# A decoder block on one core: where the rotation tables are worked out and which queues move the gate rows

## The chip, the cores and the metric

One core of a Trainium2 chip (trn2) runs the whole program. The metric is device time in microseconds (us), as the median of three runs of the kernel. Engines are named as in the profile: PE (TensorE, matrix products), DVE (VectorE), ACT (ScalarE), POOL (GpSimd) and SP (SyncE, which here only issues DMAs). Each engine works through its own queue of instructions in order and waits there for what an instruction needs; DMAs are issued from the queues of SP, ACT and POOL.

## The reference

One layer of a decoder, for 512 tokens of width 1024. The parts that matter here:

```
mod = silu(c) @ w_ada + b_ada            # six rows of 1024: shift, scale, gate, twice
h = rms_norm(x, norm1_g) * (1.0 + scale1) + shift1
z = h @ w_in                             # u, v, q, k, v, indexer q, k, weights, two gates
...
def partial_rope(x, pos, rot_dim):
    inv_freq = ROPE_THETA ** (-arange(0, rot_dim, 2) / rot_dim)
    ang = pos[..., None] * inv_freq
    cos, sin = jnp.cos(ang), jnp.sin(ang)
    ...                                  # rotate the first rot_dim columns of each head
...
x = x + gate1 * (merged @ w_out)
h2 = rms_norm(x, norm2_g) * (1.0 + scale2) + shift2
f_g, f_u = jnp.split(h2 @ w_ffn_in, 2, axis=-1)
x = x + gate2 * ((jax.nn.silu(f_g) * f_u) @ w_ffn_out)
return rms_norm(x, final_norm_g)
```

The rotation is applied to q, k and to the queries and keys of the indexer, which come out of the first products. The angles are positions times frequencies, brought into the range of the sine by taking off multiples of two pi. The gates are rows of 1024 numbers; each is used by all tokens.

## The kernel before, in words

Every product is computed with the operands split into a high and a low half (`hi`, `lo`), as three matmuls: high by high, high by low, low by high. ACT makes the high half by a copy, VectorE or POOL the low half by a subtraction.

**Order of the work.** The program is written out by hand in the order in which each engine shall take its instructions; nothing reorders them. `stream` is a list of weight chunks (`add_w`) and of rows of `w_ada` (`add_m`), in the order in which they are used. `ensure(n)` issues the loads of entries as far as their buffers allow (three raw chunks ahead, eight rows of `w_ada` ahead) and prepares entries up to n: for a weight chunk the high half (line 125) and the low half (129, or later through `do`, line 127), for a row of `w_ada` a dot product with silu(c) on VectorE (line 196), whose sum lands in a column of shifts, scales or gates.

**Prologue (lines 453 to 494).** ACT takes silu of `c`; PE spreads it over all partitions into two PSUM banks (`pc`); VectorE copies them to `scb` in SBUF (line 480). For each of the four token tiles ACT sums the squares of x (471), POOL makes the reciprocal root (356, 357), the first 256 columns are scaled (477 on VectorE, 475 on ACT for the last tile) and transposed by PE. The row factors are also spread over a bank, which ACT copies to `rbs` (490).

**First loop (lines 498 to 532).** It runs over the eight 128-row pieces kt of the transposed, modulated input, and accumulates k and six tiles of q in the eight PSUM banks. For piece kt PE does 8 matmuls high by high (512), 8 low by high (514) and 8 with the low half of the input (516), which VectorE makes at line 499. Beside them the next piece is prepared: VectorE scales it with `rbs` (504) and takes its two dot products (196); ACT multiplies the scale by the norm's gain (446, `stage_G`) and forms the high half and the full piece (450, 451, `stage_E`); VectorE then takes the low half of the weights (127). `load_xk` brings in the pieces themselves, four ahead.

**Rotation angles.** `chain` (lines 366 to 381) is a list of 26 operations on a tile of 128 by 128 (`ropes`), all on POOL, issued in one go ahead of the loop (`run_chain`, line 486). `sines()` (388), called at the end of kt = 1, makes two more operations on VectorE (389, 390) and three sines on ACT (391 to 393). Behind it POOL issues the 26 DMAs that spread the sines over the tables `tab_i` and `tab_q` (399, 402, 532).

**Middle part.** The remaining input products, the indexer's scores and the choice of keys, the two mixers and their projections; `w_ada`'s further rows are taken along between weight chunks.

**Gate rows.** When the eight dot products of a gate section (2 or 5) are done, `sec_tasks` (419 to 433) transposes the column of sums on PE, copies it on ACT (430), writes it to DRAM (`gdr`, 431) and reads it back as a row for all partitions (`gate`, 433); both DMAs are on POOL's queue. For section 2 this falls into the gate projections, at about 262 us, for section 5 into step 10 of the FFN loop.

**Later parts.** After attention, `opt_b` with `W_PB` and, woven into it, the preparation of the output product (`o_issue`, `o_step`); the output product with the first gated residual; the FFN's input products in 18 steps (lines 1603 to 1679), each with loads issued two steps ahead by SP (`s_issue`); and the last product (`zprod`), whose weights are sums of blocks that POOL's queue builds in DRAM during the FFN loop by accumulating DMAs (`wstep`, 298 and 300).

## Time and profile before

| | |
|---|---|
| median of 3 runs | 802.95 us (802.52 to 804.84) |
| profiled execution | 804.23 us |
| its span on the core | 802.5 us |
| PE busy | 783.7 us (98%) |
| DVE busy | 647.2 us (81%) |
| ACT busy | 424.0 us (53%) |
| POOL busy | 194.4 us (24%) |
| mean granted clock of TensorE | 0.989 |
| moved by DMA | 144.60 MB, mean 180 GB/s |

The span runs from the first instruction to the last on the core; the device time of the same execution is a little longer. A busy share is a mean over stages with different limits, and PE's matmuls are pipelined with modelled ends, so 98% does not say that PE works at its peak. In a row of the timeline stand the start and the length in us, the engine, the line of the kernel, the operation, what it writes and reads, and, where the engine stood idle before it, for how long and whose end released it. A row of the waits gives the waiting instruction, the one that it waited for, the total in us, the number of waits and the longest. A row of the stretches gives busy time and number of instructions of each engine, the granted clock, the mean share of the DMA engines and what they moved.

### The profile page before, as it was taken

How to read it: one execution, taken by the hardware profiler on the slowest of the kernel's cores; microseconds unless marked ns; L12 is line 12 of the kernel's file. 1: busy time of each engine (PE TensorE's matmuls, PEld its weight loads, DVE VectorE, ACT ScalarE, POOL GpSimd, SP SyncE). 2: the span in 40 equal slices, each digit the busy share in tenths (PEclk: the TensorE clock that was granted, in tenths of full speed). 3: DMA queues.
4: the chain of work that ended last, by engine and by line, in shares of the span. 5: the costliest groups of instructions: out<-in, count | busy, mean ns of one | idle time of the engine just before them, and what ended most of it. 6: DMA issues, size and time to landing. Idle time of an engine off the chain costs nothing.

```text
span 802.5 us, 12218 instructions
## 1 busy us (share of the span) xinstructions
PE 783.7 (98%) x4599; PEld 692.2 (86%) x4599; DVE 647.2 (81%) x1074; ACT 424.0 (53%) x755; POOL 194.4 (24%) x236
## 2 busy tenths in 40 slices
PE   8799999999999999999999999999999999999996
PEld 6579988888888888988888889999999999878885
DVE  5585967698888848887697778989999888798886
ACT  5446545332232327665636477555566566566653
POOL 6851043463344421000010000312221223100001
PEclk8899999999999999999999999999999999999998
DMA  9865454332346571138692603888989887656753
GB/s 362 346 201 146 112 174 123 106 94 90 105 158 208 189 232 53 53 108 264 207 246 42 209 1 105 231 238 267 269 250 244 217 219 208 185 189 201 231 181 142
DMA packets 87181, 144.60 MB, mean 180 GB/s; under 512 B 6737, under 2 KB 54625, under 8 KB 86930
## 3 DMA queue, kind: packets, MB, share of 16 engines
q1 hardware_dynamic: 75040, 111.92, 42.5%
q0 software_dynamic: 11216, 30.88, 16.4%
q10 hardware_dynamic: 866, 1.02, 0.4%
q8 instruction: 36, 0.59, 0.3%
q14 instruction: 23, 0.19, 0.1%
HBM read 139.73 MB, written 25.17 MB: 205 GB/s over the span
## 4 chain that ended last, share of the span: by engine, by line
PE 77%; DVE 8%; ACT 5%; DMA 4%; POOL 3%; issue 2%; SPq 0%; POOLq 0%; DVEq 0%; ACTq 0%
PE pb L67 8%; PE pb L66 8%; PE pb L68 8%; PE R L66 6%; PE R L68 6%; PE R L67 6%; PE pfo L67 3%; PE pfo L66 3%; PE pfo L68 3%; PE pgb L66 2%; PE pgb L67 2%; PE pgb L68 2%; PE pav L66 2%; PE pav L67 2%; PE pav L68 2%
## 5 line engine op out<-in xcount | busy, mean ns | idle before, releaser
L125 ACT ACTIVATE hi<-raw 128x1024 fp32r<-128x1024 f32 (+1 forms) x105 | 107.8, 1029 | 91.3 <-PE pb L67 20.9
L129 DVE TENSOR_TENSOR lo<-raw,hi 128x1024 fp32r<-128x1024 f32 (+2 forms) x69 | 80.5, 1168 | 28.7 <-ACT hi L125 28.6
L129 POOL TENSOR_TENSOR lo<-raw,hi 128x1024 fp32r<-128x1024 f32 x29 | 73.3, 2529 | 91.0 <-ACT hi L125 60.2
L66 PE MATMUL pb<-h,hi 128*128 128x512 f32 (+1 forms) x176 | 67.4, 383 | 0.0
L68 PE MATMUL pb<-h,lo 128*128 128x512 f32 (+1 forms) x176 | 66.8, 379 | 0.0
L67 PE MATMUL pb<-h,hi 128*128 128x512 f32 (+1 forms) x176 | 66.8, 379 | 0.0
L67 PE MATMUL pfo<-lo,za 128*128 128x512 f32 (+1 forms) x144 | 55.8, 388 | 1.4 <-DVE lo L129 1.4
L66 PE MATMUL pfo<-hi,za 128*128 128x512 f32 (+1 forms) x144 | 55.4, 384 | 0.0
L68 PE MATMUL pfo<-hi,za 128*128 128x512 f32 (+1 forms) x144 | 55.3, 384 | 0.0
L196 DVE CUSTOM_DVE_ANT_0 mraw<-mraw,scb,cols 128x1024 f32<-128x1024 f32 x27 | 39.3, 1457 | 15.0 <-DMA mraw<-in_w_ada_t_dram 15.0
L66 PE MATMUL R<-tb,sx 128*128 128x256 f32 x160 | 45.0, 281 | 0.6 <-ACT R L1637 0.3
L67 PE MATMUL R<-tb,sx 128*128 128x256 f32 x160 | 44.3, 277 | 0.0
L68 PE MATMUL R<-tb,sx 128*128 128x256 f32 x160 | 44.2, 276 | 0.0
L68 PE MATMUL R<-tb,lo 128*128 128x256 f32 x160 | 44.2, 276 | 0.0
L66 PE MATMUL R<-tb,hi 128*128 128x256 f32 x160 | 44.2, 276 | 0.0
L67 PE MATMUL R<-tb,hi 128*128 128x256 f32 x160 | 44.2, 276 | 0.0
L318 POOL COPY sm<-sm 128x1 f32<-128x1 f32 x36 | 23.7, 659 | 78.6 <-ACT sm L317 78.6
L298 POOL DMA_DIRECT2D wsum<-in_w_ffn_out_dram x24 | 21.2, 884 | 82.4 <-DMA wsum<-wsum 46.7
L68 PEld LDWEIGHTS pb<-h,lo 128*128 128x128 f32 x176 | 33.0, 188 | 5.7
L66 PEld LDWEIGHTS pb<-h,hi 128*128 128x128 f32 x176 | 33.1, 188 | 5.5
L67 PEld LDWEIGHTS pb<-h,hi 128*128 128x128 f32 x176 | 33.1, 188 | 5.3
L67 PEld LDWEIGHTS pfo<-lo,za 128*128 128x128 f32 x144 | 27.1, 188 | 8.3 <-DVE lo L129 3.2
(375 smaller groups left out, 2571.7 us busy)
## 6 DMA issues: line engine op xcount, KB each, us to landing
raw<-in_w_ffn_in_dram SPq DMA_DIRECT2D x44, 512.0 KB, 6.0
raw<-in_w_in_dram SPq DMA_DIRECT2D x38, 512.0 KB, 3.7
wsum<-in_w_ffn_out_dram POOLq DMA_DIRECT2D x30, 512.0 KB, 7.6
mraw<-in_w_ada_t_dram SPq DMA_DIRECT2D x27, 512.0 KB, 3.6
raw<-wsum SPq DMA_DIRECT2D x20, 512.0 KB, 4.0
s<-in_w_ada_t_dram SPq DMA_DIRECT2D x16, 512.0 KB, 8.8
raw<-in_w_ffn_out_dram SPq DMA_DIRECT2D x16, 512.0 KB, 4.4
wsum<-wsum POOLq DMA_DIRECT2D x10, 512.0 KB, 6.0
```

Source lines behind the costliest of these rows:

```text
L66: T.matmul(o, wh, rh, start=start, stop=False, **kw)
L67: T.matmul(o, wh, rlo, start=False, stop=False, **kw)
L68: T.matmul(o, wlo, rh, start=False, stop=stop, **kw)
L125: A.activation(hi[:, :m], e["raw"][:, :m], AF.Copy)
L129: e["lo"].tensor_sub(lo[:, :m], e["raw"][:, :m], f(hi[:, :m]))
L196: V.tensor_tensor_reduce(out=raw, in0=raw, in1=scb, scale=1.0, scalar=bias, op0=OP.mult, op1=OP.add, accum_out=col)
L298: P.dma_start(wsum[n][o], src, accum_op=OP.add)
L318: P.tensor_copy(t, t)
```

## The change

- The chain of rotation angles runs on VectorE, not POOL. The seven pairs of multiply and add become one fused operation each, and the two operations of `sines()` join the chain, which so has 21 entries. It is no longer issued in one go: four entries ahead of the first tile's scaling, four and three behind the first and second tile's, then 4, 4 and up to 8 at the ends of kt = 0, 1 and 2.
- `sines()` and the table DMAs come at the end of kt = 3, not 1.
- The first dot product reads silu(c) from the two PSUM banks, as two halves; the second half takes the first one's sum as its start. `scb` is copied by ACT, in the turn of the fourth tile, and no longer by VectorE. The first dot product is issued in the turn of the third tile.
- The copy to `rbs` stands between the two operations of `stage_E(0)`, no longer ahead of `stage_G(0)`.
- A gate row is written to DRAM from ACT's queue, in `sec_tasks`. It is read back from SP's queue by a function of its own, `gate_fetch`: for section 2 after attention, ahead of `o_issue`, for section 5 at the end of step 12 of the FFN loop.

```diff
@@ -187,14 +187,17 @@
     Gc = tiny.tile([128, 2, 16], F32, name="Gc")
     GG = {2: tiny.tile([128, 8], F32, name="GG2"), 5: tiny.tile([128, 8], F32, name="GG5")}
 
+    pc = []
+
     def dot(sec, kt, col, bias, after=lambda: None):
 
         def dma(raw):
             SY.dma_start(raw, w_ada_t[sec * D + kt * 128:sec * D + (kt + 1) * 128, :])
 
         def fn(raw):
-            V.tensor_tensor_reduce(out=raw, in0=raw, in1=scb, scale=1.0, scalar=bias, op0=OP.mult, op1=OP.add,
-                                   accum_out=col)
+            for o, c in ((slice(0, 512), pc[0]), (slice(512, D), pc[1])) if (sec, kt) == (0, 0) else ((slice(0, D), scb),):
+                V.tensor_tensor_reduce(out=raw[:, o], in0=raw[:, o], in1=c, scale=1.0,
+                                       scalar=col if o.start else bias, op0=OP.mult, op1=OP.add, accum_out=col)
             after()
         return dma, fn
 
@@ -365,20 +368,21 @@
     posf, ang, nh, nl, t0 = R[:, 0], R[:, 1], R[:, 2], R[:, 3], R[:, 4]
     chain = []
     ch = chain.append
-    ch(lambda: P.tensor_copy(posf, posi))
-    ch(lambda: P.tensor_scalar(ang, posf, freq, None, op0=OP.mult))
-    ch(lambda: P.tensor_scalar(nl, ang, float(1.0 / (2 * math.pi)), MAGIC, op0=OP.mult, op1=OP.add))
-    ch(lambda: P.tensor_scalar(nl, nl, -MAGIC, None, op0=OP.add))
-    ch(lambda: P.tensor_scalar(nh, nl, MAGIC * 2048.0, None, op0=OP.add))
-    ch(lambda: P.tensor_scalar(nh, nh, -MAGIC * 2048.0, None, op0=OP.add))
-    ch(lambda: P.tensor_sub(nl, nl, nh))
+    ch(lambda: V.tensor_copy(posf, posi))
+    ch(lambda: V.tensor_scalar(ang, posf, freq, None, op0=OP.mult))
+    ch(lambda: V.tensor_scalar(nl, ang, float(1.0 / (2 * math.pi)), MAGIC, op0=OP.mult, op1=OP.add))
+    ch(lambda: V.tensor_scalar(nl, nl, -MAGIC, None, op0=OP.add))
+    ch(lambda: V.tensor_scalar(nh, nl, MAGIC * 2048.0, None, op0=OP.add))
+    ch(lambda: V.tensor_scalar(nh, nh, -MAGIC * 2048.0, None, op0=OP.add))
+    ch(lambda: V.tensor_sub(nl, nl, nh))
     for pi, which in ((0, nh), (0, nl), (1, nh), (1, nl), (2, nh), (2, nl), (3, nh)):
-        ch(lambda pi=pi, which=which: P.tensor_scalar(t0, which, -TWO_PI[pi], None, op0=OP.mult))
-        ch(lambda: P.tensor_add(ang, ang, t0))
+        ch(lambda pi=pi, which=which: V.scalar_tensor_tensor(ang, which, -TWO_PI[pi], ang, op0=OP.mult, op1=OP.add))
     for cmp, sgn in ((OP.is_gt, -1.0), (OP.is_lt, 1.0)):
-        ch(lambda cmp=cmp, sgn=sgn: P.tensor_scalar(t0, ang, -sgn * math.pi, sgn * 2 * math.pi, op0=cmp, op1=OP.mult))
-        ch(lambda: P.tensor_add(ang, ang, t0))
-    ch(lambda: P.tensor_scalar(ang, ang, 3.1415925, -3.1415925, op0=OP.min, op1=OP.max))
+        ch(lambda cmp=cmp, sgn=sgn: V.tensor_scalar(t0, ang, -sgn * math.pi, sgn * 2 * math.pi, op0=cmp, op1=OP.mult))
+        ch(lambda: V.tensor_add(ang, ang, t0))
+    ch(lambda: V.tensor_scalar(ang, ang, 3.1415925, -3.1415925, op0=OP.min, op1=OP.max))
+    ch(lambda: V.scalar_tensor_tensor(nl, ang, -1.0, ang, op0=OP.mult, op1=OP.max))
+    ch(lambda: V.tensor_scalar(nl, nl, -1.0, math.pi / 2, op0=OP.mult, op1=OP.add))
     sn = mid.tile([128, 4, 128], F32, name="sn", tag="A2", bufs=1)
     tab = {"i": mid.tile([128, 2, S], F32, name="tab_i", tag="G2", bufs=1),
            "q": mid.tile([128, 2, S], F32, name="tab_q", tag="G3", bufs=1)}
@@ -386,8 +390,6 @@
     P.memset(tab["i"][:, 1], 0.0)
 
     def sines():
-        V.scalar_tensor_tensor(nl, ang, -1.0, ang, op0=OP.mult, op1=OP.max)
-        V.tensor_scalar(nl, nl, -1.0, math.pi / 2, op0=OP.mult, op1=OP.add)
         A.activation(sn[:, 0:3:2], nl[:, None, :].to_broadcast([128, 2, 128]), AF.Sin)
         A.activation(sn[:, 1], ang, AF.Sin, scale=-1.0)
         A.activation(sn[:, 3], ang, AF.Sin)
@@ -428,9 +430,11 @@
             T.transpose(p[:8, :128], GG[sec], ident)
             gr = tiny.tile([128, 128], F32, name="gr", tag="gr", bufs=1)
             A.activation(gr[:8], p[:8, :128], AF.Copy)
-            P.dma_start(gdr[sec], gr[:8])
-            g = gate_b[1 if sec == 2 else 2] = base.tile([128, D], F32, name="gate", tag="gate", bufs=1)
-            P.dma_start(g, rows_bcast(gdr[sec], D))
+            A.dma_start(gdr[sec], gr[:8])
+
+    def gate_fetch(sec):
+        g = gate_b[1 if sec == 2 else 2] = base.tile([128, D], F32, name="gate", tag="gate", bufs=1)
+        SY.dma_start(g, rows_bcast(gdr[sec], D))
 
     mbank = [7]
 
@@ -445,9 +449,10 @@
         o = slice(kt, kt + 1)
         A.activation(G1[:, 1, o], G1[:, 1, o], AF.Copy, scale=n1c[:, o])
 
-    def stage_E(kt, src):
+    def stage_E(kt, src, between=lambda: None):
         g, sh = G1[:, 1, kt:kt + 1], G1[:, 0, kt:kt + 1]
         A.activation(hT[kt][0], src, AF.Identity, scale=g, bias=sh)
+        between()
         A.activation(xk[kt], src, AF.Identity, scale=g, bias=sh)
 
     warm = bank(0, "warm")
@@ -458,7 +463,7 @@
 
     TURNED = 2
     keep_warm(7)
-    pc = [bank(k, "silu") for k in (0, 1)]
+    pc.extend(bank(k, "silu") for k in (0, 1))
     A.activation(crow[0:1], crow[0:1], AF.Silu)
     for h in range(2):
         o = slice(512 * h, 512 * h + 512)
@@ -471,26 +476,29 @@
         A.activation(junk, xt[i], AF.Square, accum_out=r1[:, i:i + 1])
         rstd(r1[:, i:i + 1], r1[:, i:i + 1], 1, 1.0 / D)
         xs = xt[i][:, :128 * TURNED]
+        if i == 0:
+            run_chain(4)
         if i == 3:
+            for h in range(2):
+                A.activation(scb[:, 512 * h:512 * h + 512], pc[h], AF.Copy)
             A.activation(xs, xs, AF.Copy, scale=r1[:, i:i + 1])
         else:
             V.tensor_scalar(xs, xs, r1[:, i:i + 1], None, op0=OP.mult)
-        if i == 0:
-            for h in range(2):
-                V.tensor_copy(scb[:, 512 * h:512 * h + 512], pc[h])
+        if i < 2:
+            run_chain(4 - i)
+        if i == 2:
+            ensure(W1M[0])
         o = slice(i * 128, (i + 1) * 128)
         for kt in range(TURNED):
             T.transpose(px[kt][:, o], xt[i][:, kt * 128:(kt + 1) * 128], ident)
         T.matmul(rb[:, o], r1[:, i:i + 1].to_broadcast([128, 128]), ident, start=True, stop=True)
         keep_warm(1 if i < 3 else 4)
-    run_chain(len(chain))
     rbs = base.tile([128, 512], F32, name="rbs", tag="acc", bufs=2)
     ensure(W1M[1])
     A.activation(xk[1], px[1], AF.Copy)
-    A.activation(rbs, rb, AF.Copy)
     stage_G(0)
     ensure(W1[0])
-    stage_E(0, px[0])
+    stage_E(0, px[0], lambda: A.activation(rbs, rb, AF.Copy))
     stream[W1[0]]["do"]()
     outs = [bank(m, f"o{m}") for m in range(8)]
     pk, pq = outs[:2], outs[2:]
@@ -518,9 +526,10 @@
             stage_G(kt + 1)
             stage_E(kt + 1, xk[kt + 1])
             stream[W1[kt + 1]]["do"]()
+            run_chain((4, 4, 8, 0, 0, 0, 0)[kt])
         else:
             ensure(W_Q[0][1])
-        if kt == 1:
+        if kt == 3:
             sines()
             triu = mid.tile([128, 2, 128], F32, name="triu", tag="ql", bufs=2)[:, 0]
             SY.dma_start(triu, consts[:, 128:256])
@@ -1187,6 +1196,7 @@
             wstep()
 
     mbank[0] = 5
+    gate_fetch(2)
     o_issue("B11", "B12", "B22")
     for g in range(4):
         opt_b(W_PB[g], 8, yb, ((2, 3), (0, 1), (6, 7), (0, 1))[g], pb_evac(g), None, None, None, o_step,
@@ -1674,6 +1684,8 @@
         if q == 10:
             mbank[0] = 6
             sec_tasks(True)
+        if q == 12:
+            gate_fetch(5)
         wstep()
         if q in (9, 13, NQ - 2):
             a_sum("S1", {9: 0, 13: 2}.get(q, 1))
```

## The prediction

> **What bounds the kernel now.** The page comes first, then the whole run's waits of PE, then stretches of time, then the instructions in order of time around the one long wait.
>
> ```profile
> span 802.5 us, 12218 instructions
> PE 783.7 (98%) x4599; PEld 692.2 (86%) x4599; DVE 647.2 (81%) x1074; ACT 424.0 (53%) x755; POOL 194.4 (24%) x236
> ```
>
> TensorE (PE) is busy for 783.7 of 802.5 us. What is left outside its work is 18.8 us, so every edit must be worth something in those, or nothing. PE's waits by cause show where most of it can still be won:
>
> ```profile
> PE o L516 <- DVE h L499: 4.0, 1, 4.0
> PE pfo L67 <- DVE lo L129: 1.4, 3, 0.7
> ```
>
> One wait of 4.0 us, in the first projection loop (lines 498 to 532), is larger than all others. The stretches around it (start and end, length, busy time of PE, PEld, DVE, ACT, POOL, granted clock, DMA share, GB/s):
>
> ```profile
> 5.00:15.60 10.60, 9.08 (x38) 6.75 (x36) 6.87 (x13) 7.47 (x15) 7.00 (x12) 0.71 1.03 418
> 21.50:27.10 5.60, 5.60 (x25) 4.32 (x24) 5.40 (x7) 2.23 (x4) 5.17 (x6) 1.00 1.02 413
> 27.10:35.10 8.00, 3.98 (x17) 2.92 (x16) 1.18 (x5) 1.43 (x4) 5.83 (x12) 0.89 1.03 419
> 35.10:39.30 4.20, 3.78 (x9) 2.48 (x9) 4.11 (x6) 2.28 (x6) 3.89 (x7) 0.50 0.43 159
> ```
>
> From 27.1 to 35.1 us PE works for 3.98 of 8.00 us, VectorE (DVE) for 1.18, ScalarE (ACT) for 1.43; only POOL is busy, 5.83. The timeline says with what:
>
> ```profile
> 12.17 0.99 POOL L368 CAST ropes<-posi 128x128 f32<-128x128 int32 x1
> 33.58 0.29 POOL L381 TENSOR_SCALAR ropes<-ropes 128x128 f32<-128x128 f32 x1
> 33.90 0.29 DVE L389 SCALAR_TENSOR_TENSOR ropes<-ropes 128x128 f32<-128x128 f32 x1 [6.78 <-POOL ropes L381]
> 34.23 0.23 DVE L390 TENSOR_SCALAR ropes<-ropes 128x128 f32<-128x128 f32 x1
> 34.37 0.68 DVE L499 TENSOR_TENSOR h<-xT,h 128x512 fp32r<-128x512 f32 x1
> 35.11 3.78 PE L516 MATMUL o<-h,hi 128*128 128x512 f32 x8 [4.04 <-DVE h L499]
> ```
>
> The rotation angles are a chain of POOL operations from 12.17 to 33.87. VectorE runs its queue in order, reached L389 of `sines()` 6.78 us before the chain was done, and behind it stood L499, the low half of the third input tile, for which PE stood still. So the bound here is POOL's chain, through VectorE's queue.
>
> The loop has a second, calmer bound. L446 (ACT) opens each tile kt, so its starts are the loop's beat; these are tiles 0, 1, 2, 4 and 7:
>
> ```profile
> 14.50 0.29 ACT L446 ACTIVATE G<-G,cols 128x1 f32<-128x1 f32 x1
> 19.67 0.29 ACT L446 ACTIVATE G<-G,cols 128x1 f32<-128x1 f32 x1 [2.00 <-DVE G L196]
> 25.93 0.29 ACT L446 ACTIVATE G<-G,cols 128x1 f32<-128x1 f32 x1 [3.32 <-DVE G L196]
> 43.86 0.29 ACT L446 ACTIVATE G<-G,cols 128x1 f32<-128x1 f32 x1 [2.82 <-DVE G L196]
> 57.43 0.69 DVE L499 TENSOR_TENSOR h<-xT,h 128x512 fp32r<-128x512 f32 x1 [0.92 <-ACT xT L451]
> 61.17 0.29 ACT L446 ACTIVATE G<-G,cols 128x1 f32<-128x1 f32 x1 [2.82 <-DVE G L196]
> 62.36 2.11 PE L512 MATMUL o<-h,hi 128*128 128x512 f32 x8
> ```
>
> Undisturbed, a beat is (61.17 - 43.86) / 3 = 5.77 us: L446, L450, L451 on ACT, then L499, L504 and two dot products (L196) on VectorE, then L446 again. PE follows this ring and does not set it (L512 of tile 7 starts 62.36 - 61.17 = 1.19 after its L446). VectorE has 0.92 us free per beat, just ahead of L499. From tile 2 to tile 4 the beats took 17.93 instead of 11.54: the stall costs 6.39 us. From tile 1 to 2 it took 6.26, 0.49 too long, while POOL's chain ran beside VectorE's work.
>
> **The change part by part.** *The chain moves to VectorE.* 26 POOL operations and the two of L389 and L390 become 21 on VectorE (seven fused): 11 ahead of the loop, 4 + 4 + 2 at the ends of tiles 0, 1 and 2 (the 8 allowed there find 2). VectorE's own rows on the same tile are 0.29 for two tensors and 0.23 for one. I take start to start 0.33 (33.90 to 34.23) and 0.23. Tile 0 gets three of the first kind and one of the second, 1.22 us; tile 1 two and two, 1.12; tile 2 one and one, 0.56. They run ahead of L499, in the 0.92 free. So 0.30 + 0.20 + 0 = 0.5 us come onto the ring, and no wait for POOL remains in the loop. Late next is L451 on ACT, as in the calm beats. Ends: 0.14 per operation (34.23 to 34.37) gives nothing on the ring; 0.42, the 0.35 of a piece twice as wide (7.44, below) with a gap of 0.07, gives 1.68 - 0.92 twice, 1.5 us.
>
> *Before the loop.* The second row is the time to landing of the positions' load.
>
> ```profile
> 1.25 0.78 POOL L342 DMA_DIRECT2D posi<-in_positions_dram  x1 [0.81 <-POOLq L1868]
> DMA to landing us min/median/max: 5.4/5.4/5.4
> 7.44 0.35 DVE L477 TENSOR_SCALAR x<-x,sm 128x256 f32<-128x256 f32 x1 [1.98 <-POOL sm L357]
> 7.71 1.28 DVE L480 COPY scb<-silu 128x512 f32<-128x512 f32 x2
> 9.46 0.54 POOL L357 TENSOR_TENSOR sm<-sm,mhalf 128x1 f32<-128x1 f32 x1
> 10.52 1.28 DVE L196 CUSTOM_DVE_ANT_0 s<-s,scb,cols 128x1024 f32<-128x1024 f32 x1
> 10.73 1.48 POOL L357 TENSOR_TENSOR sm<-sm,mhalf 128x1 f32<-128x1 f32 x1
> 12.24 0.51 ACT L475 ACTIVATE x<-x,sm 128x256 f32<-128x256 f32 x1 [1.87 <-POOL sm L357]
> 14.02 0.59 ACT L490 ACTIVATE rbs<-rb 128x512 f32<-128x512 f32 x1
> 15.66 2.41 PE L512 MATMUL o<-h,hi 128*128 128x512 f32 x8
> L1003 DVE CUSTOM_DVE_ANT_0 pt<-qk,sco 128x512 f32<-128x512 f32 x8 | 5.3, 686 | 4.0 <-PE qk L68 4.0
> ```
>
> The positions land at about 1.25 + 5.4 = 6.65, inside VectorE's free 1.98 us; four operations (about 1.0) end at 7.65, 0.2 after the first scaling was due. The next four (1.1) take the place of the two copies (1.28), the next three (1.0) push the third scaling to 10.4 to 10.75. The first dot product then comes in two halves out of PSUM, 0.69 each by L1003's row (one PSUM input, same width): about 1.5 with two reads of the sum against 1.28, to 12.25; the second dot product ends at 13.55. The copies of `scb` move to ACT, 2 x 0.59 by L490's row, into its free 1.87 us. L490 goes behind L450, so tile 0's first half is ready 0.6 earlier, its second half unchanged relative to L446. If POOL's power (L357) for the fourth scaling is back from 1.48 at the 0.54 of the one before, the scaling on ACT (L475) comes behind the copies, at 12.24 - 1.87 + 1.18 = 11.55, so 0.69 earlier; with L490 out of the way (14.02 to 14.50) ACT could start L446 at 13.3. So VectorE sets it: 13.65, with 0.1 for handing over, instead of 14.50. With the 1.48 kept it would be 14.0. PE's eight first matmuls (2.41) would reach bank 6 when L451 has just left it: nothing to gain there beyond 0.85.
>
> [...]
>
> *The sum for the start and the loop.* Tile 0's L446 at 13.65. Tile 1: + 5.17 (as 14.50 to 19.67) + 0.59 (L490 now inside the ring) = 19.4. Then six beats of 5.77 and 0.5: 19.4 + 34.6 + 0.5 = 54.5 for tile 7, against 61.17. That is 6.65 us earlier, with ends 7.15 and, for dear operations, 5.6.
>
> *Loads.* The DMA share is 1.02 to 1.03 up to 35.1, so a faster loop could run into them. A beat needs three pieces of 128 x 1024 and one of 128 x 512 numbers of four bytes, 1.84 MB: at 418 GB/s 4.4 us, less than 5.77. And from 5.0 to 35.1 some 12.5 MB came; 2.1 of it for x, the rest is enough for tiles 0 to 4 and nearly 5 (1.57 each for the first two), while tile 3's dot products had not begun. That lead, about two beats, is more than the 6.65 us won. Nothing added.
>
> *Sines at tile 3.* Three ACT operations go from the second beat's end to the fourth's, where ACT is free for 2.82 us ahead of L446; nothing. The tables' DMAs on POOL's queue start about 5 us later:
>
> ```profile
> 55.31 0.54 POOL L532 DMA_DIRECT2D tab_q<-tab_q  x1 [3.53 <-DMA tab_q<-tab_q]
> L542 DVE TENSOR_TENSOR sh<-sh,tab_i x5: 557/559/692, 77.1 to 109.4; 128x384 f32<-128x384 f32 x4, 128x512 f32<-128x512 f32 x1
> ```
>
> The last is issued at about 60; the first reader of the index table comes at 77.1 - 6.65 = 70.4 and that table is filled before. Cover of some 10 us; nothing.
>
> *Gate rows.* The last row is the time to landing of the two row fetches.
>
> ```profile
> 630.76 0.61 POOL L433 DMA_DIRECT2D gate<-gdr  x1 [5.06 <-DMA gdr<-gr]
> 620.65 0.25 ACT L430 ACTIVATE gr<-mod 8x128 f32<-8x128 f32 x1
> 622.70 0.38 ACT L1645 ACTIVATE ps<-R 128x256 f32<-128x256 f32 x1 [0.61 <-PE R L68]
> DMA to landing us min/median/max: 5.8/6.3/6.9
> ```
>
> The write moves behind L430 on ACT's queue: the issue and the wait for L430's own end stand ahead of L1304 and L1637, which feed PE; bounds 0 and 0.6 (an issue took 0.61 on POOL; the 0.61 idle before L1645 takes up as much). I take 0. POOL's 5.06 us wait goes, and its sums of weight rows move up by about as much; next late there are their own DMAs. In the last stage PE waits 1.4 us for low halves (above), behind such loads: between 1.4 won and 1.4 lost, I take 0. The fetch goes to SP's queue, at step 12 ahead of the next weight load and, for section 2, ahead of `o_issue`. Both writes are then long done, so SP waits for nothing; what stands behind is loads issued two steps ahead. Nothing, if that lead holds.
>
> **The rivals.** (1) *POOL locked out at the start.* If each power has to wait until VectorE's three groups end, the scalings come after a group and a whole power (0.54): 7.65 + 0.54, then 1.1 + 0.54 and 1.0 + 0.54 with the scalings of 0.35 between, the third scaling at about 12.1 instead of 10.4, all later by 1.7. Gain 6.65 - 1.7 = 4.95: 798.0. For it L357's 1.48; against it that the groups are gaps between short operations. (2) *VectorE has no room.* In 21.5 to 27.1 it was busy 5.40 of 5.60. If every operation in the loop adds in full, 2.9 us come onto the ring instead of 0.5: gain 4.25, 798.7. Against it: the 0.92 before L499 are waits for ACT. This is also the case in which the "idle time" isn't there. (3) *The tail gains.* PE's 1.4 us in the last stage go as well: 794.9. (4) *Slower: the fetch in SP's queue holds up FFN weights.* 6.3 us of landing time ahead of one step's load; PE would stand 6.3 us and then run cold, as after 35.1 (3.78 for eight matmuls at a clock of 0.50, so some 2 more): 8.3 against 6.65, 804.6. It decides only if a load has no lead at all; no PE wait for a load in the table above speaks for it.
>
> **How the numbers follow.** The profiled execution took 804.23 us, 1.73 beyond its span and 1.28 above the median of 802.95. 804.23 - 6.65 = 797.6 for a profiled run; the median, by the same shift, 802.95 - 6.65 = 796.3. Chances: this forecast 0.68, POOL locked out 0.12, no room 0.07, tail 0.09, slower 0.04. The range goes from 794.4 (the cheap end, 7.15, with the tail's 1.4) to 798.8 (no room on VectorE); the slower rival is outside. A measurement of this kernel tells about 0.3% (2.4 us) from no change. Rivals 1 to 3 and the forecast all pass it; with something kept for a mishap on top of rival 1 or 2: faster 0.92, same 0.05, slower 0.03.
>
> **What would show it.** In the new profile: no wait of PE at L516 for L499; POOL nearly empty between 12 and 35 us; the clock at 1.00 from about 20 us on; L446 beats of 6.1, 6.0 and then 5.77; L512 of tile 7 at about 55.7; the first L512 at about 14.8 with the last L357 back at some 0.54; the waits of the last stage as before. It is wrong if L499 waits longer than 0.3 for chain operations, if L477 waits for POOL or for the positions, if PE waits for loads in the FFN, or if the 6.65 us of the first 62 are given back later.

## The result and the profile after

The changed kernel takes 795.83 us (median of four runs, 795.30 to 797.38), the kernel before in the same four rounds 803.89 (802.52 to 805.44): a ratio of 0.9902, 95% interval 0.9877 to 0.9928. The forecast was 796.3 with 794.4 to 798.8. Run again beside other kernels it gave 794.46 against 805.89, a ratio of 0.9886 (0.9848 to 0.9923). The profiled execution took 795.69 us against 804.23, so 8.5 less where 6.65 were forecast. It lies inside the range, but not because each step was right: the loop came as forecast and the start did not, and some 2 us of the difference between the two profiles lie behind the loop, where no run shows that the change made them. That the median came within 0.5 us of the forecast is in part luck.

Line numbers have moved: L389 and L390 of `sines()` are now L384 and L385 of the chain, L446, L450, L451 of ACT are L450, L454, L456, L499 is L507, L504 is L512, and L512, L516 of PE are L520, L524. First the page, then PE's waits:

```profile
span 793.9 us, 12210 instructions
PE 782.8 (99%) x4599; PEld 692.8 (87%) x4599; DVE 649.7 (82%) x1093; ACT 424.9 (54%) x757; POOL 176.4 (22%) x206
...
PE pfo L67 <- DVE lo L129: 0.5, 2, 0.3
PE o L520 <- ACT h L454: 0.3, 1, 0.3
```

The wait of 4.0 us at the first loop's L516 has gone; what is left in the loop is one wait of 0.3. PE's busy time is the same within 1 us, so the gain is time in which PE stood still. Two of the stretches shown before, in the same columns:

```profile
27.10:35.10 8.00, 7.86 (x33) 6.22 (x34) 7.41 (x16) 4.66 (x7) 0.00 (x0) 1.00 1.04 419
35.10:39.30 4.20, 4.17 (x18) 3.13 (x18) 3.55 (x5) 1.69 (x3) 0.00 (x0) 1.00 1.03 416
```

From 27.1 to 35.1 PE works 7.86 us of 8.00 (3.98 before), POOL nothing (5.83 before), and the granted clock stays at 1.00 where it had fallen to 0.89 and, in the stretch behind it, to 0.50. The beat of the loop is read from L450, and the place of its end from PE's first matmul of tile 7 (timeline; tiles 0, 1, 2, 3, 4 and 7):

```profile
14.69 0.29 ACT L450 ACTIVATE G<-G,cols 128x1 f32<-128x1 f32 x1
20.11 0.29 ACT L450 ACTIVATE G<-G,cols 128x1 f32<-128x1 f32 x1 [2.22 <-DVE G L199]
25.98 0.29 ACT L450 ACTIVATE G<-G,cols 128x1 f32<-128x1 f32 x1 [2.93 <-DVE G L199]
31.78 0.29 ACT L450 ACTIVATE G<-G,cols 128x1 f32<-128x1 f32 x1 [2.86 <-DVE G L199]
37.54 0.30 ACT L450 ACTIVATE G<-G,cols 128x1 f32<-128x1 f32 x1 [2.82 <-DVE G L199]
...
54.84 0.29 ACT L450 ACTIVATE G<-G,cols 128x1 f32<-128x1 f32 x1 [2.82 <-DVE G L199]
56.04 2.14 PE L520 MATMUL o<-h,hi 128*128 128x512 f32 x8
```

Beats of 5.42, 5.87, 5.80 and then 5.77 us. Tile 7's first matmul starts at 56.04 instead of 62.36: 6.32 us earlier. The first beat opens at 14.69, not at the 13.65 forecast; before it was 14.50. The timeline of VectorE, ACT and POOL shows what holds it:

```profile
10.73 0.75 DVE L199 CUSTOM_DVE_ANT_0 s<-s,silu,cols 128x512 f32<-128x512 f32 x1
10.93 0.55 POOL L360 TENSOR_TENSOR sm<-sm,mhalf 128x1 f32<-128x1 f32 x1
11.52 0.60 ACT L483 ACTIVATE scb<-silu 128x512 f32<-128x512 f32 x1 [0.94 <-DVE G L199]
11.63 0.75 DVE L199 CUSTOM_DVE_ANT_0 s<-s,silu,G 128x512 f32<-128x512 f32 x1
12.42 0.60 ACT L483 ACTIVATE scb<-silu 128x512 f32<-128x512 f32 x1 [0.30 <-DVE G L199]
12.91 0.50 ACT L484 ACTIVATE x<-x,sm 128x256 f32<-128x256 f32 x1
13.05 1.28 DVE L199 CUSTOM_DVE_ANT_0 s<-s,scb,cols 128x1024 f32<-128x1024 f32 x1 [0.67 <-ACT scb L483]
14.19 0.60 ACT L498 ACTIVATE xT<-xT 128x512 f32<-128x512 f32 x1 [0.78 <-PE xT L493]
```

Each copy of `scb` on ACT waits for a half of the dot product on VectorE (0.94 and 0.30 us), although neither writes what the other reads: both read the same bank of PSUM. Each copy starts 0.04 us after its half has ended (10.73 + 0.75 = 11.48 and 11.63 + 0.75 = 12.38). Why a read waits for a read is not shown; whether it waits goes with the order of the two in the program (runs 5, 9 and 12). ACT's scaling (L484), in ACT's queue behind them, comes at 12.91 instead of the 11.55 forecast, and the second dot product waits 0.67 us for the copies. L450 follows the copy of the transposes (L498, 14.19) without a wait, so in this trace the fourth input tile ends last.

### The profile page after: what moved, and what is told of

Same layout as the page of the kernel before. It is cut to its first block, busy times and chain, and to the rows that moved or that the text cites. A ratio compares the mean times of both kernels' runs of the same rounds, so it can differ in the third digit from the quotient of the medians.

```text
span 793.9 us, 12210 instructions
## 1 busy us (share of the span) xinstructions
PE 782.8 (99%) x4599; PEld 692.8 (87%) x4599; DVE 649.7 (82%) x1093; ACT 424.9 (54%) x757; POOL 176.4 (22%) x206
## 4 chain that ended last, share of the span: by engine, by line
PE 85%; DVE 8%; ACT 3%; DMA 2%; issue 1%; POOL 0%; POOLq 0%; SPq 0%; ACTq 0%; DVEq 0%
PE pb L68 8%; PE pb L67 8%; PE pb L66 8%; PE R L66 7%; PE R L67 7%; PE R L68 7%; PE pfo L67 4%; PE pfo L66 4%; PE pfo L68 4%; PE pgb L66 2%; PE pgb L67 2%; PE pgb L68 2%; PE pav L67 2%; PE pav L66 2%; PE pav L68 2%
## 5 line engine op out<-in xcount | busy, mean ns | idle before, releaser
L67 PE MATMUL pb<-h,hi 128*128 128x512 f32 (+1 forms) x176 | 66.8, 379 | 0.0
L67 PE MATMUL pfo<-lo,za 128*128 128x512 f32 (+1 forms) x144 | 55.5, 385 | 0.5 <-DVE lo L129 0.5
L321 POOL COPY sm<-sm 128x1 f32<-128x1 f32 x36 | 27.5, 763 | 86.3 <-ACT sm L320 86.3
L67 PE MATMUL R<-tb,hi 128*128 128x256 f32 x160 | 44.4, 278 | 0.0
L67 PE MATMUL R<-tb,sx 128*128 128x256 f32 x160 | 44.4, 277 | 0.0
L67 PEld LDWEIGHTS pb<-h,hi 128*128 128x128 f32 x176 | 33.1, 188 | 5.4
L67 PEld LDWEIGHTS pfo<-lo,za 128*128 128x128 f32 x144 | 27.1, 188 | 6.6 <-DVE lo L129 1.4
```

Of the source, the lines that this page charges most:

```text
L67: T.matmul(o, wh, rlo, start=False, stop=False, **kw)
L321: P.tensor_copy(t, t)
```

## The experiments

**1. The chain alone** (`e1`): the kernel before with the chain on VectorE in the change's slots and the sines at tile 3; start and gate rows as before.

```
-    ch(lambda: P.tensor_scalar(ang, posf, freq, None, op0=OP.mult))
+    ch(lambda: V.tensor_scalar(ang, posf, freq, None, op0=OP.mult))
...
-    run_chain(len(chain))
...
+            run_chain((4, 4, 8, 0, 0, 0, 0)[kt])
...
-        if kt == 1:
+        if kt == 3:
             sines()
```

> The kernel before with the chain of angles on VectorE in the same places as in the change and the sines at tile 3; the start (dot products from scb, copied by VectorE, rbs ahead of the loop) and the gate rows are as before. Theory A (the 6.3 us won by tile 7 are the stall alone, and the 1.5 to 2.2 us that the changed kernel's trace gains further on come from POOL no longer waiting for the gate row): 6.3 us less than before, about 797.6. Theory B (the chain is all of it, and the later gains are scatter between executions): the same as the changed kernel, about 795.8.

Measured: 795.76 us (794.50 to 800.63) against 803.18, ratio 0.9910 (0.9882 to 0.9939). This part alone is worth as much as the whole change, within what can be measured. Its first beat opens later, at 15.82, and tile 7's first matmul at 56.70.

**2. The gate rows alone** (`e2`).

```
-            P.dma_start(gdr[sec], gr[:8])
-            g = gate_b[1 if sec == 2 else 2] = base.tile([128, D], F32, name="gate", tag="gate", bufs=1)
-            P.dma_start(g, rows_bcast(gdr[sec], D))
+            A.dma_start(gdr[sec], gr[:8])
...
+    gate_fetch(2)
...
+        if q == 12:
+            gate_fetch(5)
```

> The kernel before with the gate rows alone moved to the queues of ScalarE and SP. Theory A: POOL's sums of weight rows run about 6 us earlier and PE's waits in the last stage fall from 1.4 us to 0.5: 1 to 1.5 us less than before, about 802.4. Theory B: no change, 803.9. A fetch that holds up the FFN's loads in SP's queue would make it slower.

Measured: 802.57 us against 803.18, ratio 0.9993 (0.9973 to 1.0014): no change that can be measured, as forecast. The interval runs from 2.2 us less to 1.1 us more, so theory A's gain of 1 to 1.5 us is not excluded; PE's wait in the last stage fell from 1.4 to 1.0 us, not to 0.5.

**3. The sines later, the chain still on POOL** (`e3`): one line.

```
-        if kt == 1:
+        if kt == 3:
             sines()
```

> The kernel before with one edit: the sines and the table DMAs at tile 3 instead of tile 1; the chain stays on POOL. POOL ends it at about 34 us and VectorE reaches L389 at about 39, so it waits for nothing. Theory C (what cost was the wait in VectorE's queue, not the engine of the chain): the 6.39 us of the stall go, less some 0.5 us a beat for up to three beats in which POOL's operations draw VectorE's out: about 5.3 less than before, 798.6. Theory D (the chain has to leave POOL): a wait of some us stays in the loop, above 801.

Measured: 798.51 us, ratio 0.9937 (0.9914 to 0.9961). So moving the wait by two beats, which costs no work at all, brings 4.7 us by the medians (3.1 to 6.9 by the interval), where run 1 brought 7.4. What it leaves is seen in VectorE's timeline (low halves of tiles 1 to 4, and the operation that had waited 6.78 us):

```profile
22.30 0.81 DVE L499 TENSOR_TENSOR h<-xT,h 128x512 fp32r<-128x512 f32 x1 [0.67 <-ACT xT L451]
28.50 0.82 DVE L499 TENSOR_TENSOR h<-xT,h 128x512 fp32r<-128x512 f32 x1 [0.66 <-ACT xT L451]
34.71 0.96 DVE L499 TENSOR_TENSOR h<-xT,h 128x512 fp32r<-128x512 f32 x1 [0.66 <-ACT xT L451]
40.11 0.28 DVE L389 SCALAR_TENSOR_TENSOR ropes<-ropes 128x128 f32<-128x128 f32 x1
...
41.11 0.69 DVE L499 TENSOR_TENSOR h<-xT,h 128x512 fp32r<-128x512 f32 x1 [0.46 <-ACT xT L451]
```

L389 waits no more: POOL's chain, now drawn out to 37.97, ends 2.1 us before VectorE reaches L389. In this run the same low half takes 0.81 to 0.96 us while POOL works on the chain, after it 0.69, and the beats are 6.2 to 6.4 (starts at 20.27, 26.48, 32.69 and 39.08) instead of 5.77. POOL's rows are stretched too: in the trace of before its additions on the chain take 0.82 to 1.08 us while VectorE works beside them (17 to 27 us), and 0.45 to 0.46 while VectorE stands still. Why the rows of both are longer there is not shown.

**4. The start undone** (`e4`): the changed kernel with VectorE's copies of `scb`, the whole dot product from SBUF, and `rbs` ahead of `stage_G(0)` again.

```
-            for o, c in ((slice(0, 512), pc[0]), (slice(512, D), pc[1])) if (sec, kt) == (0, 0) else ((slice(0, D), scb),):
...
+            V.tensor_tensor_reduce(out=raw, in0=raw, in1=scb, scale=1.0, scalar=bias, op0=OP.mult, op1=OP.add,
+                                   accum_out=col)
...
-                A.activation(scb[:, 512 * h:512 * h + 512], pc[h], AF.Copy)
...
+                V.tensor_copy(scb[:, 512 * h:512 * h + 512], pc[h])
```

> The changed kernel with its start as before: VectorE copies scb, the first dot product reads it from SBUF in one piece, rbs is copied ahead of the loop. The prediction had the new start worth 0.85 us, so 796.7. The trace of the changed kernel shows L446's successor at 14.69 against 14.50 before, so by that the start is worth nothing: 795.8, within 0.3.

Measured: 796.06 us, ratio 0.9911 (0.9883 to 0.9940). The time is the same. The trace is finer: the first beat opens at 15.79 as in run 1, so the new start does win 1.1 us at that point against the chain with the old start; by tile 7 0.6 of it is left (56.67 against 56.04).

**5. The copies before the halves** (`e5`).

```
+        if i == 2:
+            for h in range(2):
+                A.activation(scb[:, 512 * h:512 * h + 512], pc[h], AF.Copy)
         A.activation(junk, xt[i], AF.Square, accum_out=r1[:, i:i + 1])
...
         if i == 3:
-            for h in range(2):
-                A.activation(scb[:, 512 * h:512 * h + 512], pc[h], AF.Copy)
```

> The changed kernel, except that ScalarE's two copies of scb stand ahead of the square of the third input tile, and so ahead of the two halves of VectorE's first dot product, which read the same banks of PSUM. Theory P (the start gained nothing because the copies had to follow the halves): the second dot product no longer waits 0.67 us for scb, the first L450 comes at about 13.7 us instead of 14.69 and the first L520 about 0.9 earlier; the run is 0.8 to 1.0 us below the changed kernel (about 794.9 median), if the square that comes later stays hidden. Theory Q (the start is set by the power of the fourth sum on POOL and the scaling behind it, or by the transposes): the first L450 stays at 14.5 or later and the time stays at 795.8.

Measured: 794.56 us, ratio 0.9884 (0.9844 to 0.9925), not to be told from the changed kernel. First L450 at 14.18, between the two theories (in an execution in which PE's spreading of silu(c) took 1.98 us; 14.54 in one of the changed kernel with 2.09, run 11). The wait for the copies is gone, but the copies now stand ahead of the third square, which comes at 9.04 instead of 8.17 and takes everything behind it along:

```profile
8.09 1.06 ACT L478 ACTIVATE scb<-silu 128x512 f32<-128x512 f32 x2
9.04 1.06 ACT L479 ACTIVATE junk<-x 128x1024 f32<-128x1024 f32 x1
```

**6. More operations on the ring** (`e6`): the changed kernel with 2, 4, 8 and 8 further operations of VectorE, on a slice that nothing reads, at the ends of tiles 3 to 6.

```
             run_chain((4, 4, 8, 0, 0, 0, 0)[kt])
+            for j in range((0, 0, 0, 2, 4, 8, 8)[kt]):
+                V.scalar_tensor_tensor(R[:, 5], R[:, 5] if j else nl, 1.0, ang, op0=OP.mult, op1=OP.max)
```

> The changed kernel with 2, 4, 8 and 8 more operations of VectorE, like those of the chain, on an unused slice of the ropes tile, at the ends of tiles 3, 4, 5 and 6. It measures what an operation costs where the chain was put. Theory A (as predicted: 0.92 us are free in a beat, 0.33 to an operation): the beats behind them are 5.77, 6.2, 7.5 and 7.5. Theory B (as the chain's own beats show it, 5.87 and 5.80: an operation takes 0.31 and about 1.15 are free): 5.77, 5.87, 7.1, 7.1. In both every operation above the free time counts in full. A beat that is longer already behind two operations would speak against both.

Measured, VectorE's groups with the low half behind each, and L450 of tiles 4 to 7:

```profile
38.41 0.61 DVE L531 SCALAR_TENSOR_TENSOR ropes<-ropes 128x128 f32<-128x128 f32 x2
39.42 0.69 DVE L507 TENSOR_TENSOR h<-xT,h 128x512 fp32r<-128x512 f32 x1 [0.40 <-ACT xT L456]
44.18 1.27 DVE L531 SCALAR_TENSOR_TENSOR ropes<-ropes 128x128 f32<-128x128 f32 x4
45.36 0.68 DVE L507 TENSOR_TENSOR h<-xT,h 128x512 fp32r<-128x512 f32 x1
50.11 2.57 DVE L531 SCALAR_TENSOR_TENSOR ropes<-ropes 128x128 f32<-128x128 f32 x8
52.60 0.68 DVE L507 TENSOR_TENSOR h<-xT,h 128x512 fp32r<-128x512 f32 x1
```

```profile
37.40 0.29 ACT L450 ACTIVATE G<-G,cols 128x1 f32<-128x1 f32 x1 [2.82 <-DVE G L199]
43.16 0.29 ACT L450 ACTIVATE G<-G,cols 128x1 f32<-128x1 f32 x1 [2.11 <-DVE G L199]
49.09 0.29 ACT L450 ACTIVATE G<-G,cols 128x1 f32<-128x1 f32 x1 [2.99 <-DVE G L199]
56.33 0.29 ACT L450 ACTIVATE G<-G,cols 128x1 f32<-128x1 f32 x1 [4.30 <-DVE G L199]
```

Beats of 5.76, 5.93 and 7.24 behind 2, 4 and 8 operations. Four take 1.18 us up to the low half, eight 2.49, so 0.30 to 0.31 each; the beats grow by 0.16 and 1.47 over 5.77. Both give the same free time, 1.18 - 0.16 = 1.02 and 2.49 - 1.47 = 1.02. Neither theory had the pair right; the second's beats (5.87 and 7.1) come nearer than the first's (6.2 and 7.5). The single run took 800.87 us, of which these operations explain the 1.6 at tile 7; more of the rest below.

**7. The dot products ahead of the low half** (`e7`): this opens the ring.

```
     for kt in range(8):
+        if kt < 7:
+            ensure(W1M[2 * kt + 3])
         V.tensor_sub(hT[kt][1], xk[kt], f(hT[kt][0]))
...
-            ensure(W1M[2 * kt + 3])
```

> The changed kernel with the two dot products of the next tile issued ahead of the low half (L507) of the present one, so that L450 of the next tile no longer waits for the whole of VectorE's work. Theory R (the loop's beat of 5.77 is the ring through ACT and VectorE): the ring opens, PE's own work or VectorE's sets the beat at 5.45 to 5.55, tile 7 comes 1.5 to 2.2 us earlier and the median is about 794. Theory S (VectorE's sum of work or the loads set the beat, the ring only follows): the beat stays within 0.05 of 5.77 and the time at 795.8. A loss can come from L507 itself: behind the dot products it reaches PE later, so waits of PE at L524 for h may take the place of what is won.

Measured: 792.48 us (790.54 to 795.22), ratio 0.9858 (0.9824 to 0.9892), the lowest median of the study; its interval overlaps that of the changed kernel. PE's timeline, tiles 6 and 7 (the first row lacks the first of its eight matmuls, which began at 48.51):

```profile
48.74 1.75 PE L521 MATMUL o<-h,hi 128*128 128x512 f32 x7
50.32 1.98 PE L523 MATMUL o<-h,lo 128*128 128x512 f32 x8
52.14 1.98 PE L525 MATMUL o<-h,hi 128*128 128x512 f32 x8
53.95 1.98 PE L521 MATMUL o<-h,hi 128*128 128x512 f32 x8
```

Three groups, each 1.81 us after the one before, make a beat of 5.44: PE itself now sets the loop, and from 21.5 to 50 it is busy throughout (28.50 of 28.50 us). Tile 7 begins at 53.95, 2.09 earlier than in the changed kernel. The ring was the loop's bound.

**8. Both** (`e8`): the edits of runs 5 and 7 together.

> The copies ahead of the halves and the dot products ahead of the low half, both. If theories P and R hold and what they win is kept to the end, the two sums add up: some 2.5 us below the changed kernel, 793.3. If the loads set the loop once the start is earlier, less than the sum: 794 or more.

Measured: 794.95 us, ratio 0.9886 (0.9851 to 0.9920). They do not add up: the first L450 came at 15.23, later than in either (14.18 and 14.55). The second copy had to wait for PE's spreading of silu(c), and with it the third square (10.10). Here that spreading took 3.75 us, in run 5's execution 1.98, so this delay comes from the early copies together with a slow spreading, not from joining the two edits:

```profile
9.60 0.60 ACT L478 ACTIVATE scb<-silu 128x512 f32<-128x512 f32 x1 [1.11 <-PE silu L470]
```

**9. The copies behind the third square** (`e9`, and **10**, `e10`, with the dot products of run 7). The edit is shown against run 5.

```
-        if i == 2:
+        if i == 3:
             for h in range(2):
                 A.activation(scb[:, 512 * h:512 * h + 512], pc[h], AF.Copy)
```

> The changed kernel with ScalarE's copies of scb one place later than in the run before: behind the square of the third input tile and ahead of the fourth's, so that they still come before the dot halves and no longer push the third square. Theory P (order of the copies and the halves, with room for the copies only behind the third square): halves at about 10.7 to 12.3, second dot product right behind them, first L450 at 13.7 to 13.9 against 14.69, whether the broadcast of c on TensorE takes 2.0 or 3.75 us; the time 0.8 to 0.9 us below the changed kernel run beside it. Theory Q (something else holds the start: the fourth tile's power, the weights' conversion, the first rows): L450 at 14.2 or later, time unchanged within 0.3.

> The same place of the copies, and the two dot products ahead of the low half in the loop. If both parts add: tile 7's first matmul 0.9 + 2.2 us ahead of the changed kernel's 57.33, at about 54.2, and the median 3 us below the changed kernel run beside it. If the loads set the loop once it is this early, waits of TensorE or VectorE for raw weights show and less than 2.5 us is left.

(57.33 is the start of the sixth of tile 7's eight matmuls; the first starts at 56.04. The same holds for the 55.08 of run 7 in the last run's expectation; the first starts at 53.95.)

Measured: 796.75 us, ratio 0.9911 (0.9876 to 0.9946), and 795.32, ratio 0.9899 (0.9857 to 0.9941). Both missed, by a mistake in the edit: the halves are issued in the step of the third input tile, so at `i == 3` the copies still follow them in the program. They wait as before, and now the fourth square waits behind them:

```profile
11.50 0.60 ACT L478 ACTIVATE scb<-silu 128x512 f32<-128x512 f32 x1 [2.19 <-DVE G L199]
...
12.90 1.05 ACT L479 ACTIVATE junk<-x 128x1024 f32<-128x1024 f32 x1
```

The first L450 is at 16.91. The miss shows the order at work all the same: ACT was ready 2.19 us earlier, both banks were filled by 9.56 (the spreading of silu(c) began at 5.81 and took 3.75), and the copy still waited for the half that stood ahead of it in the program.

**11. The changed kernel once more** (`e11`).

> The changed kernel, not altered, once more. It tells apart two readings of the stretches in which TensorE's 256-wide matmuls follow each other every 118 ns instead of 113 (560 to 612 us in the first profile of this kernel). If they belong to the program, they lie at 560 to 612 again; if they belong to the single execution, they lie elsewhere or are missing, and the span moves by 0.04 us for each us of such a stretch. The broadcast of c (3.75 us there, 2.07 in the profile of before) should in the same way be long or short with the first L450 staying at 14.5 to 14.7. Median expected: 795.8 within 0.8.

Measured: 794.46 us, ratio 0.9886 (0.9848 to 0.9923), and a profile that is 3.0 us shorter (span 790.9) though the kernel is the same: L450 at 14.54, tile 7 at 55.90, and no stretch of 118 ns at 560 to 612. The spreading of silu(c) took 2.09 us instead of 3.75.

**12. The copies really ahead of the halves, with run 7's dot products** (`e12`): the copies at `i == 2`, just ahead of `ensure(W1M[0])`.

> The dot products ahead of the low half, and ScalarE's copies of scb issued behind the third square but, in the program, ahead of the dot halves (which are issued in the third input tile's step, so that in the two runs before the copies still stood behind them). Theory P: an access of a bank waits for the accesses of the other engine that stand ahead of it in the program, and for nothing else. Then the copies run at about 9.2 to 10.2 us without a wait for VectorE, the halves at 10.7 to 12.3, the second dot product ends at 13.6, and the first L450 comes at 13.7 to 13.9; with the loop as in the run of the dot products alone, tile 7's first matmul at about 54.2 against its 55.08. Against the changed kernel about 3 us in a profile without stretches of 118 ns, and a ratio to before of 0.985. Theory Q: what holds the start is not this order; then the first L450 stays at 14.2 or later.

Measured: 793.59 us, ratio 0.9870 (0.9845 to 0.9895), the same as run 7 within the intervals. The order was mended and the start hardly moved:

```profile
9.32 1.06 ACT L489 ACTIVATE scb<-silu 128x512 f32<-128x512 f32 x2
10.28 1.06 ACT L476 ACTIVATE junk<-x 128x1024 f32<-128x1024 f32 x1
12.37 0.51 ACT L482 ACTIVATE x<-x,sm 128x256 f32<-128x256 f32 x1 [0.94 <-POOL sm L360]
12.40 1.28 DVE L199 CUSTOM_DVE_ANT_0 s<-s,scb,cols 128x1024 f32<-128x1024 f32 x1
12.98 0.62 PE L462 MATMUL warm<-ones 128*128 128x128 f32 x2
13.41 0.41 PE L493 MATMUL xT<-ident,x 128*128 128x128 f32 x2
13.86 0.60 ACT L498 ACTIVATE xT<-xT 128x512 f32<-128x512 f32 x1 [0.98 <-PE xT L493]
14.35 0.29 ACT L450 ACTIVATE G<-G,cols 128x1 f32<-128x1 f32 x1
```

The copies wait for nobody, and VectorE's second dot product starts at 12.40 instead of 13.05 and has its sum at 13.69, where theory P wanted it. Still L450 comes at 14.35, behind the copy of the fourth tile's transposes (L498), which had waited 0.98 us for PE. The fourth tile was scaled by 12.88 (L482), but PE turned it only at 13.41: its pairs of small matmuls (transposes, spreading of the row factors, warming) had followed each other every 0.43 us without a gap since 9.52, right behind the long spreading of silu(c). Theory Q holds for this start: behind VectorE's way there is a second one, through PE's own queue, and in run 7, with the copies where the change has them, PE came to the same transposes at 13.39.

## Why the prediction was right, and where it was not

**The stall: right.** POOL's chain, through VectorE's queue, cost 6.39 us in the trace of before; in the trace of after no wait is in its place, and run 1, which has only that part, gives the whole gain. Run 3 adds what the prediction did not separate: at tile 7 (first matmul; before's start in all three) run 2 stands at 62.89, run 3 at 57.58 and run 1 at 56.70. So 5.31 us came from where the wait stood, and 0.88, net, from POOL no longer working beside VectorE: run 1 had paid 0.8 more by the time of its first beat and some 0.1 in the ring.

**The ring: right in kind, two sizes off.** Forecast were 0.30 and 0.20 us in the second and third beats, measured 0.10 and 0.03. The chain's four operations of tile 0 take 1.11 us, not 1.22: the last, a single-input one, gives way after 0.14.

```profile
21.13 0.94 DVE L379 SCALAR_TENSOR_TENSOR ropes<-ropes 128x128 f32<-128x128 f32 x3
22.10 0.23 DVE L381 TENSOR_SCALAR ropes<-ropes 128x128 f32<-128x128 f32 x1
22.24 0.69 DVE L507 TENSOR_TENSOR h<-xT,h 128x512 fp32r<-128x512 f32 x1
```

And the free time is 1.02 by run 6, where the profile's idle time had given 0.92. 1.11 - 1.02 = 0.09 is the measured 0.10; tile 1's four (27.00 to 28.05) give 0.03.

**The start: wrong.** The step that failed is "the copies of `scb` move to ACT, 2 x 0.59, into its free 1.87 us". ACT was free, but the copies followed VectorE's halves, each 0.04 us after its half had ended. The other parts of that step held: the halves took 0.75 each (0.69 forecast), POOL's last power fell from 1.48 to 0.55, and the powers ahead took 0.63, 0.56 and 0.60 beside the chain's first eleven operations, so rival 1 did not come. For the last power's return to 0.54 before's trace had one row: beside VectorE's copies out of PSUM (7.71 to 8.99) a power took 0.55 (from 8.02). Beside the whole dot product out of SBUF it took 1.48, 1.46 and 1.47 (before, runs 2 and 3), beside a half out of PSUM 0.55 (the changed kernel, run 11); why is not shown.

What this order costs by itself is seen in run 11, where the spreading of silu(c) was short: PE stands still for 1.18 us until L484 has scaled the fourth tile, and L450 comes at 14.54. Where the spreading is long, as in the changed kernel's first profile, PE's own queue is nearly as late: by the same steps of 0.43 it could have taken the fourth tile's transposes at 13.40 (worked out from 12.97), and it took them at 13.47. So in such an execution 13.65 was out of reach even with the order mended (run 12: VectorE ready at 13.69, L450 at 14.35). The prediction put PE's part of the start at nothing; it read it from before's profile, which has the short spreading and in which PE waited 0.80 us for ACT there. No run has the copies ahead of the halves and behind the third square in an execution with the short spreading, so whether 13.65 can be reached there stays open.

The figure that 13.65 was set against was off as well. Before's profile opens its loop at 14.50, but runs 2 and 3, with the same start, at 15.03: in their executions PE's spreading of silu(c) took 3.75 us and VectorE's second copy waited for it, in before's it took 2.07. Against 15.03 the change starts 0.34 earlier, made up of 0.8 lost to the chain's operations (15.8 in runs 1 and 4) and 1.1 won by the new start.

**Tile 7's first matmul: 55.7 forecast, 56.04 and 55.90 measured.** In the profiles shown, 6.32 us are gained instead of 6.65. Against the forecast the start lost 1.04, the first beat gave 0.34 back (5.42 where 5.17 + 0.59 were forecast) and the ring 0.37. Against run 2, which has before's start and the same long spreading, the gain is 62.89 - 56.04 = 6.85. That the sum came out so near is luck in part: an error of 1.04 at the start was met by two smaller ones, 0.34 and 0.37, the other way. The first L520 itself came at 15.84, not at the 14.8 forecast.

**Loads, sines, gate rows: right.** No wait of PE for a load shows in the loop, not even with run 7's beat of 5.44. The sines at tile 3 run at 39.44 to 40.24 in ACT's free time. The gate rows are worth nothing that run 2 could measure; POOL's 5.06 us wait is gone.

**What was kept: all of it.** From tile 7 to the start of the second norm, PE takes 404.7 to 404.9 us in all fourteen profiles. The rest of the 8.6 us of span lies behind that point (worked out from the starts of the same matmul in both traces, us):

```
                       before   after   again (run 11)
first matmul, tile 7    62.36   56.04    55.90
second norm             11.2    10.2      9.8
FFN, both products     206.9   207.9    206.6
turn to the last stage  23.6    23.1     22.0
last stage to the end   93.5    91.8     91.8
```

Of these 2.3 us, 1.7 lie in the last row. Run 3, whose code there is before's, takes 92.5, so 1.0 of them came and went without any edit. From tile 7 to PE's last matmul the fourteen profiles range from 727.8 us (run 7) to 735.1 (run 3), so 2.3 us between two of them cannot be put down to the change. "Tail waits as before" was wrong for this pair (1.4 us to 0.5 at L67), but the wait is 1.0 in run 2 (gate rows moved), 0.5 in run 1 and 2.7 in run 3 (not moved), and missing in runs 7 and 11 (moved). That the moved rows shorten it is possible and not shown.

## What to carry to other kernels

A wait for another engine costs what stands behind it in the queue, so ask first where it stands: one line that moved the sines by two beats was worth 5.31 of the 6.19 us that the chain's move won by tile 7 (runs 2, 3 and 1). In a loop held by a ring, an operation counts only beyond the ring's free time, which a few dummy operations measure (1.02 us in a beat of 5.77, run 6); and opening the ring (here the dot products ahead of the low half) won another 2.09 us by tile 7. An engine's idle time may be no room for a read of a PSUM bank that another engine reads too: ACT's copies waited for VectorE where they stood behind the halves in the program (0.94 and 0.30 us in the changed kernel, 2.19 and 0.30 in run 9) and not where they stood ahead (runs 5 and 12). Before moving work into a start, follow the second-latest way to its end, in more than one execution.

## What the runs showed of the hardware

TensorE's 256-wide matmuls of the FFN follow each other every 113 ns, and in stretches every 118 ns, with the granted clock at 1.00 and PE busy in both. Eleven successive ones in the changed kernel, and eleven in run 7 (first and last of each):

```profile
590.93 0.28 PE L66 MATMUL R<-h,hi 128*128 128x256 f32 x1
...
592.11 0.28 PE L67 MATMUL R<-h,hi 128*128 128x256 f32 x1
```

```profile
590.07 0.28 PE L66 MATMUL R<-h,sa 128*128 128x256 f32 x1
...
591.20 0.28 PE L67 MATMUL R<-tb,sx 128*128 128x256 f32 x1
```

Ten steps take 1.18 and 1.13 us. The long slower stretches begin at different times and end where one of the two products ends (about 612 or 685): 560 to 612 in the first profile of the changed kernel, not there in the second; 550 to 687 in run 12 and 500 to 685 in run 6, whose FFN took 212.0 and 212.3 us instead of 206.6. That is most of what run 6 lost beyond its ring. They belong to the execution and not to the program, since the same kernel has them or not, and they take up to 5.7 us, against some 8 that this change brings. What causes them stays open: no difference in loads, waits or granted clock was found that goes with them.

The spreading of silu(c), four matmuls, takes 1.95 to 2.09 us in four of the fourteen profiles and 3.75 to 3.77 in the other ten (2.09 and 3.75 in two of the changed kernel), while the clock column has 1.00 for 5.8 to 7.9 in both. PE's next rows show that the clock column misses something. Where the spreading was short (before, run 11), a pair of 128-wide matmuls takes 0.39 us at 8.5 and 0.63 or 0.64 from about 9.6 on, and the column has 0.50 for 9.6 to 12.0. Where it was long (the changed kernel, run 7), the same pairs take 0.63 to 0.64 from the first one at 10.0 on, and in the changed kernel's trace the column still has 1.00 for 9.6 to 15.0. So both kinds have a stretch in which PE is slow; in the long kind it begins earlier, with the spreading, and the column does not show it. Why it begins earlier stays open. Which of the two it is moves the old start by 0.5 us (14.50 and 15.03) and the changed start by 0.15 or less (14.54; 14.69 and, in run 7, 14.55).
